# Indexer and attention scores of a hybrid decoder layer: the low product of two heads on 64 rows each

## The chip, the cores and the metric

The kernel runs on one core of a Trainium2 chip. The metric is the device time of one execution in microseconds; lower is better. The kernel before took 1328.76 us, the median of 3 runs (1328.71 to 1334.23).

A core has TensorE (PE, matrix products; its weight loads are listed as PEld), VectorE (DVE), ScalarE (ACT), GpSimd (POOL), and SyncE (SP), which issues the DMAs here. Products land in PSUM banks, from which ACT and DVE read.

## The reference

One decoder layer on 1024 tokens with 16 learned meta tokens ahead, width 1024. A root-mean-square norm feeds one input projection, whose columns go to two mixers side by side: chunkwise retention with 4 heads, and sparse attention. Their outputs are concatenated and projected, added to the input, and a squared-ReLU MLP follows. Everything is float32. The part that matters here is the sparse attention, block by block of 128 queries:

```python
s = einsum('bchd,bsd->bchs', iqb, ikf)              # indexer: 8 heads of 64, one shared key
score = einsum('bch,bchs->bcs', iwb, relu(s))       # weighted sum over the heads
_, sel = top_k(where(causal, score, NEG), 256)      # 256 keys for each query
logits = einsum('bchd,bckd->bchk', qb, k_sel)       # attention: 8 heads of 64, shared keys
p = softmax(where(valid, logits + bias, NEG))       # bias by distance, 32 buckets
out = einsum('bchk,bckd->bchd', p, v_sel)
```

## The kernel before

**Two halves.** Each float32 operand of a large product is split into a high half (rounded to the reduced format fp32r that PE takes) and a low half (the rest). A projection is then three products: high x high, low x high, high x low (L229 to L231).

**Stacked scores.** The heads of the indexer and of the attention have 64 entries, half of PE's 128 rows, so the kernel stacks. The key tiles hold the high half twice, in rows 0-63 and 64-127 (`ikh`, `knh`), and likewise the low half (`ikl`, `knl`; `stacks`, L273 to L275). A query tile of one head has its high half in one set of 64 rows and its low half in the other. Which is where alternates: for even heads the high half is in rows 0-63, for odd heads in rows 64-127 (L317 to L323 for the indexer, L529 to L534 for the attention). One product with the high keys gives q_high·k_high + q_low·k_high. A second one with the low keys, into the same bank, adds q_high·k_low + q_low·k_low.

**Indexer.** `index(i, st)` (L325 to L341) runs for the query blocks 1 to 7. For each of 8 heads it goes over chunks of the 16 + 128(i+1) keys (one chunk up to 512 columns, then 2 or 3 near-equal ones): two products into one of the five banks of the pool "R" (`psB`, L332 and L333), a ReLU on ACT that scales by the head's weight (L335), and a signed sum into `sc[i]` on DVE (L337, L339). Per head, the seven blocks have 272 + 400 + 528 + 656 + 784 + 912 + 1040 = 4,592 columns in 13 chunks.

**Top-k.** It runs bit by bit on DVE and ACT, beside the retention (183 to 421 us). Afterwards `sc[i]` holds 0-or-large penalties in place of scores.

**Attention.** `attend_p(i, g)` takes block i and four heads. For each head it goes over the segments of the keys: the last 240 (with the distance bias) and the chunks before. Each segment is two products into one of three banks of the pool "A" (`psA`, L554 and L555), and one DVE operation that adds the bias or penalty and takes the minimum (L556). After the last segment comes the exponential on ACT (L563), and a `yield`, four in a call. Per head, the eight blocks have 144 + 4,592 = 4,736 columns in 18 segments. `attend_v` transposes the exponentials (L581), splits them (L587, L588) and multiplies by the values (L589, L590) with banks of the pool "R". Its first step covers only the 16 meta tokens, so that its two products have 16 rows; all other steps have 128.

**Order.** `spread` interleaves the generators of one step (scores of a unit, values of the unit before, pieces of the output projection L640 to L642) by their yields. On top of that the program is given to a planner that simulates the engines with a cost model and puts on each engine, in program order of priority, what is ready first. Each engine then runs its list in that order. The DMAs stand in SP's list.

**Memory.** `shift(pool, n)` takes n bytes of each partition out of a pool by a buffer that is only cleared once (L122).

Of the kernel before, what the change touches and what calls it, by code (L numbers as in the profile page):

```python
# [9 lines left out]
F32 = mybir.dt.float32  # L10
# [3 lines left out]
AF = mybir.ActivationFunctionType  # L14
ALU = mybir.AluOpType
# [55 lines left out]
def chunks(n, c0=0):  # L71
    k = -(-n // 512)
    out = []
    for j in range(k):
        a, b = (n * j // k) // 64 * 64, (n * (j + 1) // k) // 64 * 64 if j + 1 < k else n
        out.append((c0 + a, b - a))
    return out
# [3 lines left out]
def layer(ctx, tc, x, meta, norm1_w, w_in, ret_w, q_w, k_w, rel, w_out, norm2_w, w1, w2,  # L81
          ident_d, pack_d, hot_d, out, gam):
    nc = tc.nc
    const = ctx.enter_context(tc.tile_pool(name="const", bufs=1))
    wp = ctx.enter_context(tc.tile_pool(name="wp", bufs=1))
    small = ctx.enter_context(tc.tile_pool(name="small", bufs=2))
# [10 lines left out]
    def psA():  # L97
        return pp.tile([128, 512], F32, tag="A", name="psA", bufs=3)

    def psB():  # L100
        return pp.tile([128, 512], F32, tag="R", name="psB", bufs=5)
# [18 lines left out]
    def shift(pool, n):  # L120

        nc.gpsimd.memset(pool.tile([128, n // 4], F32, name="shift", bufs=1), 0.0)  # L122

    shift(const, 128)
    shift(small, 224)
    ident = const.tile([128, 128], F32, name="ident")
    nc.sync.dma_start(ident, ident_d)
    nrow = const.tile([128, D], F32, name="nrow", tag="nrow")
# [33 lines left out]
    ikl = px.tile([128, KW], F32R, name="ikl")  # L162
# [122 lines left out]


    ncol = [NM + 128 * (i + 1) for i in range(NB)]
    sc = [None] * NB

    def sc_tile(i, shape, dt, name):  # L290
        return kp_.tile(shape, dt, tag=f"sc{i}", name=name)
# [33 lines left out]

    def index(i, st):
        sc[i] = sc_tile(i, [128, ncol[i]], F32, "sc")
        for h in range(8):
            for c0, w in chunks(ncol[i]):
                dst = sc[i][:, c0:c0 + w]  # L330
                ps = psB()
                nc.tensor.matmul(ps[:, :w], st[:, h], ikh[:, c0:c0 + w], start=True, stop=False)  # L332
                nc.tensor.matmul(ps[:, :w], st[:, h], ikl[:, c0:c0 + w], start=False, stop=True)  # L333
                r = big.tile([128, 512], F32, tag="oh", name="rl", bufs=3)
                nc.scalar.activation(r[:, :w], ps[:, :w], AF.Relu, scale=absw[:, i, h:h + 1])  # L335
                if h == 0:
                    nc.vector.tensor_scalar(dst, r[:, :w], sgnw[:, i, h:h + 1], None, op0=ALU.mult)  # L337
                else:
                    nc.vector.scalar_tensor_tensor(dst, r[:, :w], sgnw[:, i, h:h + 1], dst, op0=ALU.mult, op1=ALU.add)  # L339
        diag = sc[i][:, ncol[i] - 128:]  # L340
        nc.gpsimd.affine_select(diag, diag, pattern=[[-1, 128]], compare_op=ALU.is_ge, fill=-BIG,  # L341
                                base=0, channel_multiplier=1)
# [9 lines left out]
    ps = psA()  # L352
# [10 lines left out]
    for b in range(NB):  # L363
        if b + 2 < NB:
            do_norm1(b + 2)
        sb = small_proj(b, sh, sl)
        key_T([(sb[:, 0:64], 128)], NM + 128 * b, ikh, ikl)
        if b == 0:
            s8 = small_proj(8, sh, sl)
            key_T([(s8[:NM, 0:64], NM)], 0, ikh, ikl)  # L370
        if b:
            index(b, index_q(b))
# [24 lines left out]
    knh = ap_.tile([128, KW], F32R, name="knh")  # L397
    knl = ap_.tile([128, KW], F32R, name="knl")
    bias = ap_.tile([128, 8, WIN], F32, name="bias")
    kr = rsqrt(kss, 9)  # L400
    for b in range(9):
        P = NM if b == 8 else 128
# [22 lines left out]
    st = {}  # L425
# [64 lines left out]
    for b in range(NB):  # L490
        ps = psA()
# [16 lines left out]
    segs = {}  # L508
    wins = {i: min(ncol[i], WIN) for i in range(NB)}
    for i in range(NB):  # L510
        n = ncol[i]
        win = wins[i]
        segs[i] = [(c0, w, False) for c0, w in chunks(n - win)] + [(n - win, win, True)]
    qst = {}
# [21 lines left out]
    def attend_p(i, g):  # L536
        n = ncol[i]
        win = wins[i]
        mb = at["m"][:, g]
        u = 2 * i + g  # L540
        nc.gpsimd.tensor_tensor(mb[:, :, :win], bias[:, 4 * g:4 * g + 4, WIN - win:],
                                sc[i][:, None, n - win:].to_broadcast([128, 4, win]), op=ALU.add)
        P = []
        sums = small.tile([128, 4], F32, name="sums")
        rs = small.tile([128, 4], F32, name="rs")
        for hh in range(4):
            per = 4 if i < 3 else 2
            if hh % per == 0:
                pp2 = (page if u < 4 or u % 4 >= 2 and i >= 3 else page_b)([128, per, n if i < 7 else 1056], F32, "P")
            p = pp2[:, hh % per]  # L550
            mn = small.tile([128, len(segs[i])], F32, name="mn", tag=f"mn{len(segs[i])}")
            for k, (c0, w, last) in enumerate(segs[i]):
                ps = psA()
                nc.tensor.matmul(ps[:, :w], qst[i][:, 4 * g + hh, :], knh[:, c0:c0 + w], start=True, stop=False)  # L554
                nc.tensor.matmul(ps[:, :w], qst[i][:, 4 * g + hh, :], knl[:, c0:c0 + w], start=False, stop=True)  # L555
                nc.vector.tensor_tensor_reduce(  # L556
                    out=p[:, c0:c0 + w], in0=ps[:, :w], in1=mb[:, hh, :win] if last else sc[i][:, c0:c0 + w],
                    scale=1.0, scalar=3e38, op0=ALU.add, op1=ALU.min, accum_out=mn[:, k:k + 1])
            m1 = mn
            if len(segs[i]) > 1:  # L560
                m1 = small.tile([128, 1], F32, name="m1")
                nc.vector.tensor_reduce(m1, mn, axis=mybir.AxisListType.X, op=ALU.min)
            nc.scalar.activation(p[:, :n], p[:, :n], AF.Exp, scale=-1.0, bias=m1, accum_out=sums[:, hh:hh + 1])  # L563
            P.append(p)
            yield
        nc.vector.reciprocal(rs, sums)
        res[i, g] = P, rs
# [100 lines left out]
    for h in range(4):  # L668
        st["w", h] = load_cols(w_in, [(o + 128 * h, 128) for o in (RQ, RK, RV, RG)])
        ret_meta(h)  # L670
        for c in range(NB):
            if h == 3 and c == 5:
                open_att()
                load_q(0)
            if h == 3 and c == 6:
                load_q(1)
            if h == 3 and c == 7:
                spread((4, attend_p(0, 0)))
            cur = ret_in(h, c)
            if prev:  # L680
                ret_out(*prev)
            prev = cur
    ret_out(*prev)
    spread((4, attend_p(0, 1)))


# [85 lines left out]
    for u in range(2, 2 * NB):  # L772
        i, g = u // 2, u % 2
        if g == 0 and i + 1 < NB:
            load_q(i + 1)
        work = [(4, attend_p(i, g))]
        if u == 2:
            work.append((2, attend_v(0, 0)))
        work.append(((u - 1) // 2 + 2, attend_v((u - 1) // 2, (u - 1) % 2)))
        for ch, b in pieces.get(u, ()):  # L780
            work.append((9, out_piece(ch, b)))
        spread(*work)
# [335 lines left out]
def build(nc, inputs):  # L1118
    arrays, args = {}, []

    def add(name, a):
        arrays[name] = a
        args.append(nc.dram_tensor(name, a.shape, mybir.dt.from_np(a.dtype), kind="ExternalInput").ap())
    for name in _INS:
        a = np.ascontiguousarray(inputs[name])
        if name in ("x", "w_in", "w_out", "w_ff1", "w_ff2"):
            a = a[0]
        add(f"in_{name}_dram", a)
    ident, pack, hot, gam = shape_constants()
    add("ident_dram", ident)  # L1130
    add("pack_dram", pack)
    add("hot_dram", hot)
    args.append(nc.dram_tensor("out_0_dram", (T, D), F32, kind="ExternalOutput").ap())
    with tile.TileContext(nc, schedule_with_timeline_sim=True) as tc:
        layer(tc, *args, gam)
    return arrays
# [10 lines left out]
```

## Time and profile before

| | |
|---|---|
| median of 3 runs | 1328.76 us (1328.71 to 1334.23) |
| profiled execution | 1329.52 us, its span 1327.7 us |
| granted TensorE clock, mean | 0.983 |
| PE busy | 1271.8 us, 6200 matmuls |
| PE weight loads busy | 1047.9 us, 6200 loads |
| DVE / ACT / POOL busy | 1076.9 / 750.4 / 260.8 us |

A busy share is that of the whole span. A matmul's recorded time runs to a modelled end and overlaps the next matmul's, so that the distance between two starts tells what a matmul costs in a row of them. A granted clock of 1.00 is 2.4 GHz, 0.50 is 1.2 GHz. Shapes of PE are given as rows x weight columns, then rows x moving columns: `128*128 128x512` has 128 rows and streams 512 columns, `16*128 16x512` has 16 rows.

### The profile page before, as it was taken

How to read it: one execution, taken by the hardware profiler on the slowest of the kernel's cores; microseconds unless marked ns; L12 is line 12 of the kernel's file. 1: busy time of each engine (PE TensorE's matmuls, PEld its weight loads, DVE VectorE, ACT ScalarE, POOL GpSimd, SP SyncE). 2: the span in 40 equal slices, each digit the busy share in tenths (PEclk: the TensorE clock that was granted, in tenths of full speed). 3: DMA queues.
4: the chain of work that ended last, by engine and by line, in shares of the span. 5: the costliest groups of instructions: out<-in, count | busy, mean ns of one | idle time of the engine just before them, and what ended most of it. 6: DMA issues, size and time to landing. Idle time of an engine off the chain costs nothing. (4 is left out here: it accounts for less than half of the span.)

```text
span 1327.7 us, 18666 instructions
## 1 busy us (share of the span) xinstructions
PE 1271.8 (96%) x6200; PEld 1047.9 (79%) x6200; DVE 1076.9 (81%) x2387; ACT 750.4 (57%) x1593; POOL 260.8 (20%) x297
## 2 busy tenths in 40 slices
PE   6999999899899999999997999999999999999998
PEld 5888868687777778787775888888888888888887
DVE  5678999899979878676759877777878988887875
ACT  6676647577753667565756555555556444444442
POOL 4004472323434424220343000000000200000000
PEclk9999999899999899999998999999999999999999
DMA  9103040202201211212362434434538844434222
GB/s 283 57 17 90 33 133 9 72 11 71 64 16 49 95 64 49 67 45 72 112 213 88 156 130 161 148 129 173 175 135 298 334 160 159 158 134 184 96 95 96
DMA packets 93664, 153.74 MB, mean 116 GB/s; under 512 B 7240, under 2 KB 47344, under 8 KB 89856
## 3 DMA queue, kind: packets, MB, share of 16 engines
q1 hardware_dynamic: 93568, 152.56, 33.5%
q8 instruction: 49, 0.80, 0.2%
q14 instruction: 47, 0.39, 0.1%
HBM read 110.58 MB, written 43.46 MB: 116 GB/s over the span
## 5 line engine op out<-in xcount | busy, mean ns | idle before, releaser
L898 ACT ACTIVATE wh<-ga 128x512 fp32r<-128x512 f32 x144 | 87.2, 628 | 158.7 <-PE psB L1046 141.5
L229 PE MATMUL psA<-wh,uh 128*128 128x512 f32 x376 | 152.4, 406 | 4.4 <-DVE gs L455 4.3
L231 PE MATMUL psA<-wl,uh 128*128 128x512 f32 x376 | 150.4, 400 | 0.0
L230 PE MATMUL psA<-wh,ul 128*128 128x512 f32 x376 | 150.1, 399 | 0.0
L899 DVE TENSOR_TENSOR wl<-ga,wh 128x512 fp32r<-128x512 f32 x144 | 96.7, 687 | 47.4 <-ACT wh L898 46.8
L898 ACT ACTIVATE wh<-sum 128x512 fp32r<-128x512 f32 x128 | 78.6, 625 | 74.3 <-DVE sum L895 69.9
L1046 PE MATMUL psB<-wh,wl 128*128 128x512 f32 x280 | 108.9, 389 | 0.0
L1047 PE MATMUL psB<-wl,wh 128*128 128x512 f32 x280 | 108.9, 389 | 0.0
L1045 PE MATMUL psB<-wh 128*128 128x512 f32 x280 | 106.8, 389 | 0.0
L689 DVE TENSOR_SCALAR_CACHE_REDUCE jk_cnt<-sc,tcand 128x400 bf16<-128x400 f32 (+1 forms) x124 | 102.2, 824 | 1.0
L694 ACT ACTIVATE jk_top<-sc,tcand 128x272 bf16<-128x272 f32 (+2 forms) x93 | 85.0, 914 | 28.2 <-DVE tcand L728 23.6
L899 DVE TENSOR_TENSOR wl<-sum,wh 128x512 fp32r<-128x512 f32 x128 | 87.7, 685 | 6.4 <-ACT wh L898 4.7
L229 PEld LDWEIGHTS psA<-wh,uh 128*128 128x128 f32 x376 | 72.2, 192 | 19.0 <-issue 3.5
L191 POOL TENSOR_TENSOR wl<-wr,wh 128x512 fp32r<-128x512 f32 x56 | 80.9, 1460 | 31.2 <-PE psB L641 15.5
L965 POOL COPY ga<-wl 128x1 f32<-128x1 f32 x8 | 6.6, 826 | 401.6 <-PE psB L928 276.2
L231 PEld LDWEIGHTS psA<-wl,uh 128*128 128x128 f32 x376 | 71.9, 191 | 14.4
L230 PEld LDWEIGHTS psA<-wh,ul 128*128 128x128 f32 x376 | 72.4, 192 | 13.5
L587 ACT ACTIVATE ph<-psB 128x512 fp32r<-128x512 f32 (+1 forms) x88 | 51.3, 592 | 48.3 <-PE psB L581 40.3
L588 DVE TENSOR_TENSOR ph<-psB,ph 128x512 fp32r<-128x512 f32 (+1 forms) x88 | 59.4, 683 | 17.4 <-ACT ph L587 15.9
L335 ACT ACTIVATE rl<-psB,absw 128x320 f32<-128x320 f32 (+5 forms) x104 | 52.7, 554 | 36.4 <-PE psB L333 23.9
L1046 PE MATMUL psA<-wh,wl 128*128 128x512 f32 x168 | 65.4, 389 | 0.0
L1047 PE MATMUL psA<-wl,wh 128*128 128x512 f32 x168 | 65.4, 389 | 0.0
(354 smaller groups left out, 3669.9 us busy)
## 6 DMA issues: line engine op xcount, KB each, us to landing
ga<-hid SPq DMA_DIRECT2D x28, 1024.0 KB, 4.9
wr<-in_w_ff_dram SPq DMA_DIRECT2D x34, 512.0 KB, 4.8
hid<-hs SPq DMA_DIRECT2D x48, 256.0 KB, 2.0
wr<-in_w_in_dram SPq DMA_DIRECT2D x32, 256.0 KB, 3.2
gb<-in_w_ff_dram SPq DMA_DIRECT2D x8, 1024.0 KB, 4.9
ga<-in_w_ff_dram SPq DMA_DIRECT2D x8, 1024.0 KB, 5.6
wr<-in_w_out_dram SPq DMA_DIRECT2D x12, 512.0 KB, 3.8
xt<-in_x_dram SPq DMA_DIRECT2D x8, 512.0 KB, 4.6
```

The source lines that it names most:

```text
L191: (nc.vector if alt and altc[0] % 2 else nc.gpsimd).tensor_tensor(shl, raw, shp.bitcast(F32), op=ALU.subtract)
L229: nc.tensor.matmul(ps[:P, :n], uh, wh, start=d == 0, stop=False)
L230: nc.tensor.matmul(ps[:P, :n], ul, wh, start=False, stop=False)
L231: nc.tensor.matmul(ps[:P, :n], uh, wl, start=False, stop=d == 7)
L588: nc.vector.tensor_tensor(pl[:kp], tp[:kp], ph[:kp].bitcast(F32), op=ALU.subtract)
L689: nc.vector.tensor_scalar(jk_[:, :ncol[i]], sc[i], cand[:, j:j + 1], 0.0, op0=ALU.is_ge, op1=ALU.add, accum_out=cnt[:, j:j + 1])
L694: nc.scalar.activation(jk_top[:, :ncol[i]], sc[i], AF.Sign, scale=-1.0, bias=cand[:, j:j + 1], accum_out=cnt[:, j:j + 1])
L898: nc.scalar.activation(view(hi), s, AF.Copy)
L899: nc.vector.tensor_tensor(view(lo), s, view(hi).bitcast(F32), op=SUB)
L1045: nc.tensor.matmul(ps[tb], ah[:, t], bh, start=j == 0 and m not in CONT, stop=False, skip_group_check=True)
L1046: nc.tensor.matmul(ps[tb], al[:, t], bh, start=False, stop=False, skip_group_check=True)
L1047: nc.tensor.matmul(ps[tb], ah[:, t], bl, start=False, stop=j == NO - 1, skip_group_check=True)
```

## The change

The second product of each chunk keeps only the 64 rows that hold the query's high half, so that q_low·k_low is no longer added. Two neighbouring heads, whose high halves lie in different sets of rows, are taken together: both high products, then both low products, then both evacuations. The second bank of a pair comes from the pool "R", in the attention too. In the attention the minima get four buffers in place of two, a yield moves into the middle of a pair's segments, and the two exponentials of a pair follow each other. The filler of the pool `small` shrinks by 192 bytes.

```diff
-    shift(small, 224)
+    shift(small, 32)
...
+    def half(h):
+
+        return slice(64 * (h % 2), 64 * (h % 2) + 64)
...
-        for h in range(8):
-            for c0, w in chunks(ncol[i]):
-                dst = sc[i][:, c0:c0 + w]
-                ps = psB()
+        for h2, c0, w in [(h, c0, w) for h in range(0, 8, 2) for c0, w in chunks(ncol[i])]:
+            dst = sc[i][:, c0:c0 + w]
+            pss = [psB(), psB()]
+            for h, ps in zip((h2, h2 + 1), pss):
                 nc.tensor.matmul(ps[:, :w], st[:, h], ikh[:, c0:c0 + w], start=True, stop=False)
-                nc.tensor.matmul(ps[:, :w], st[:, h], ikl[:, c0:c0 + w], start=False, stop=True)
+            for h, ps in zip((h2, h2 + 1), pss):
+                a = half(h)
+                nc.tensor.matmul(ps[:, :w], st[a, h], ikl[a, c0:c0 + w], start=False, stop=True)
+            for h, ps in zip((h2, h2 + 1), pss):
                 r = big.tile([128, 512], F32, tag="oh", name="rl", bufs=3)
...
-        for hh in range(4):
+        for h2 in (0, 2):
...
-            p = pp2[:, hh % per]
-            mn = small.tile([128, len(segs[i])], F32, name="mn", tag=f"mn{len(segs[i])}")
+            heads = [(hh, 4 * g + hh, pp2[:, hh % per], small.tile([128, len(segs[i])], F32, name="mn", tag=f"mn{len(segs[i])}",
+                                                                   bufs=4)) for hh in (h2, h2 + 1)]
             for k, (c0, w, last) in enumerate(segs[i]):
-                ps = psA()
-                nc.tensor.matmul(ps[:, :w], qst[i][:, 4 * g + hh, :], knh[:, c0:c0 + w], start=True, stop=False)
-                nc.tensor.matmul(ps[:, :w], qst[i][:, 4 * g + hh, :], knl[:, c0:c0 + w], start=False, stop=True)
-                nc.vector.tensor_tensor_reduce(
...
+                pss = [psA(), psB()]
+                for (hh, h, p, mn), ps in zip(heads, pss):
+                    nc.tensor.matmul(ps[:, :w], qst[i][:, h, :], knh[:, c0:c0 + w], start=True, stop=False)
+                for (hh, h, p, mn), ps in zip(heads, pss):
+                    a = half(h)
+                    nc.tensor.matmul(ps[:, :w], qst[i][a, h, :], knl[a, c0:c0 + w], start=False, stop=True)
+                for (hh, h, p, mn), ps in zip(heads, pss):
+                    nc.vector.tensor_tensor_reduce(
...
+                if k == (len(segs[i]) - 1) // 2:
+                    yield
+            for hh, h, p, mn in heads:
...
+                nc.scalar.activation(p[:, :n], p[:, :n], AF.Exp, scale=-1.0, bias=m1, accum_out=sums[:, hh:hh + 1])
+                P.append(p)
             yield
```

## Rows read from the trace of the kernel before

**Rows 1.** The page: busy time, share of the span, instructions.
```profile
PE 1271.8 (96%) x6200; PEld 1047.9 (79%) x6200; DVE 1076.9 (81%) x2387; ACT 750.4 (57%) x1593; POOL 260.8 (20%) x297
```

**Rows 2.** Busy time by stage: indexer, retention, attention; columns in the first line.
```profile
core 0: us, PE busy (x) PEld busy (x) DVE busy (x) ACT busy (x) POOL busy (x), PEclk, DMA share, GB/s
...
44.00:183.00 139.00, 136.22 (x742) 116.34 (x740) 117.74 (x245) 89.78 (x198) 48.49 (x43) 1.00 0.19 60
183.00:421.00 238.00, 222.80 (x1117) 183.01 (x1116) 221.60 (x678) 150.54 (x407) 83.83 (x122) 0.96 0.15 45
421.00:640.00 219.00, 210.56 (x1187) 169.07 (x1186) 165.63 (x554) 140.03 (x306) 65.41 (x46) 0.98 0.20 66
```

**Rows 3.** PE's waits in those three stages: us in total, times, longest.
```profile
PE psB L332 <- ACT rl L335: 2.4, 3, 1.0
...
PE psB L475 <- DVE sm L472: 10.0, 5, 3.6
...
PE psA L554 <- DVE mn L556: 1.9, 4, 0.8
```

**Rows 4.** Timeline of PE, plain runs: start us, us, instruction, shape.
```profile
672.19 0.39 PE L641 MATMUL psB<-wh,ys 128*128 128x512 f32 x1
672.41 0.39 PE L642 MATMUL psB<-wl,ys 128*128 128x512 f32 x1
672.64 0.39 PE L640 MATMUL psB<-wh,ys 128*128 128x512 f32 x1
...
106.44 0.34 PE L333 MATMUL psB<-ikl,iq 128*128 128x384 f32 x1
106.62 0.35 PE L332 MATMUL psB<-ikh,iq 128*128 128x400 f32 x1
...
486.35 0.27 PE L554 MATMUL psA<-knh,qs 128*128 128x240 f32 x1
486.46 0.27 PE L555 MATMUL psA<-knl,qs 128*128 128x240 f32 x1
```

**Rows 5.** The second products by line: count, ns min/median/max, first and last start, forms.
```profile
L333 PE MATMUL psB<-ikl,iq x104: 279/316/376, 44.8 to 182.6; 128*128 128x400 f32 x24, 128*128 128x320 f32 x24, 128*128 128x272 f32 x16, 128*128 128x256 f32 x8
...
L555 PE MATMUL psA<-knl,qs x144: 262/278/420, 421.0 to 613.1; 128*128 128x240 f32 x56, 128*128 128x288 f32 x16, 128*128 128x416 f32 x16, 128*128 128x144 f32 x8
```

**Rows 6.** Groups by line and form, the 16-row products: count, busy, mean ns, idle.
```profile
L590 PE MATMUL psB<-ph,vv 16*128 16x512 f32 x16 | 8.2, 515 | 0.1
L589 PE MATMUL psB<-ph,vv 16*128 16x512 f32 x16 | 8.2, 511 | 1.7 <-ACT ph L587 1.7
```

**Rows 7.** Timeline of PE around a 16-row product.
```profile
586.64 0.34 PE L555 MATMUL psA<-knl,qs 128*128 128x416 f32 x1
586.91 0.49 PE L589 MATMUL psB<-ph,vv 16*128 16x512 f32 x1
587.33 0.50 PE L640 MATMUL psB<-wh,ys 128*128 128x512 f32 x1
587.67 0.39 PE L641 MATMUL psB<-wh,ys 128*128 128x512 f32 x1
```

**Rows 8.** Weight loads at the same place, and their waits from 421 to 640 us.
```profile
586.91 0.18 PEld L589 LDWEIGHTS psB<-ph,vv 16*128 16x128 f32 x1 [0.27 <-ACT ph L587]
587.33 0.19 PEld L640 LDWEIGHTS psB<-wh,ys 128*128 128x128 f32 x1 [0.24 <-issue]
587.44 0.19 PEld L641 LDWEIGHTS psB<-wh,ys 128*128 128x128 f32 x1
...
PEld psB L640 <- issue: 1.9, 8, 0.2
```

**Rows 9.** Timeline of PE in the indexer, a chunk among projections.
```profile
49.07 0.41 PE L229 MATMUL psA<-wh,uh 128*128 128x512 f32 x1
49.32 0.28 PE L332 MATMUL psB<-ikh,iq 128*128 128x272 f32 x1
49.44 0.29 PE L333 MATMUL psB<-ikl,iq 128*128 128x272 f32 x1
49.57 0.40 PE L230 MATMUL psA<-wh,ul 128*128 128x512 f32 x1
```

**Rows 10.** DVE's groups for a chunk: indexer (44 to 183 us), attention.
```profile
L339 DVE SCALAR_TENSOR_TENSOR sc<-rl,sgnw,sc 128x320 f32<-128x320 f32 (+5 forms) x84 | 52.7, 664 | 9.8 <-ACT rl L335 8.8
...
L556 DVE CUSTOM_DVE_ANT_0 P<-psA,mb 128x240 f32<-128x240 f32 x56 | 22.5, 402 | 6.9 <-PE psA L555 6.7
```

**Rows 11.** Busy time and granted clock from 441 to 449 us; PE just before.
```profile
441.00:449.00 8.00, 8.00 (x30) 6.48 (x30) 5.17 (x23) 2.58 (x7) 1.64 (x1) 0.50 0.30 98
...
438.31 0.49 PE L589 MATMUL psB<-ph,vv 16*128 16x512 f32 x1
...
439.20 0.26 PE L555 MATMUL psA<-knl,qs 128*128 128x32 f32 x1
439.39 0.53 PE L590 MATMUL psB<-ph,vv 16*128 16x512 f32 x1
```

More of the change, by code (lines that the diff above doesn't have):

```diff
@@ L545, in attend_p @@
         rs = small.tile([128, 4], F32, name="rs")
-        for hh in range(4):
+        for h2 in (0, 2):
             per = 4 if i < 3 else 2
-            if hh % per == 0:
+            if h2 % per == 0:
                 pp2 = (page if u < 4 or u % 4 >= 2 and i >= 3 else page_b)([128, per, n if i < 7 else 1056], F32, "P")
-            p = pp2[:, hh % per]
-            mn = small.tile([128, len(segs[i])], F32, name="mn", tag=f"mn{len(segs[i])}")
+            heads = [(hh, 4 * g + hh, pp2[:, hh % per], small.tile([128, len(segs[i])], F32, name="mn", tag=f"mn{len(segs[i])}",
+                                                                   bufs=4)) for hh in (h2, h2 + 1)]
@@ L552, in attend_p @@
             for k, (c0, w, last) in enumerate(segs[i]):
-                ps = psA()
-                nc.tensor.matmul(ps[:, :w], qst[i][:, 4 * g + hh, :], knh[:, c0:c0 + w], start=True, stop=False)
-                nc.tensor.matmul(ps[:, :w], qst[i][:, 4 * g + hh, :], knl[:, c0:c0 + w], start=False, stop=True)
-                nc.vector.tensor_tensor_reduce(
-                    out=p[:, c0:c0 + w], in0=ps[:, :w], in1=mb[:, hh, :win] if last else sc[i][:, c0:c0 + w],
-                    scale=1.0, scalar=3e38, op0=ALU.add, op1=ALU.min, accum_out=mn[:, k:k + 1])
@@ L559, in attend_p @@
[L559 to L564, printed above, removed]
+                pss = [psA(), psB()]
+                for (hh, h, p, mn), ps in zip(heads, pss):
+                    nc.tensor.matmul(ps[:, :w], qst[i][:, h, :], knh[:, c0:c0 + w], start=True, stop=False)
@@ new lines, in attend_p @@
+                for (hh, h, p, mn), ps in zip(heads, pss):
[3 more added lines that the diff above has]
+                    nc.vector.tensor_tensor_reduce(
+                        out=p[:, c0:c0 + w], in0=ps[:, :w], in1=mb[:, hh, :win] if last else sc[i][:, c0:c0 + w],
+                        scale=1.0, scalar=3e38, op0=ALU.add, op1=ALU.min, accum_out=mn[:, k:k + 1])
@@ L565, in attend_p @@
+                if k == (len(segs[i]) - 1) // 2:
+                    yield
+            for hh, h, p, mn in heads:
+                m1 = mn
+                if len(segs[i]) > 1:
+                    m1 = small.tile([128, 1], F32, name="m1")
+                    nc.vector.tensor_reduce(m1, mn, axis=mybir.AxisListType.X, op=ALU.min)
+                nc.scalar.activation(p[:, :n], p[:, :n], AF.Exp, scale=-1.0, bias=m1, accum_out=sums[:, hh:hh + 1])
+                P.append(p)
             yield
```

## The prediction

> **What bounds the kernel now.** I read the page's busy times first, then the busy times by stage, then TensorE's order of time around the places that change. TensorE (PE) is busy for 96% of the span, VectorE (DVE) for 81% [rows 1]. The change touches two stages: the indexer's scores (44 to 183 us) and the attention's (421 to 640 us). In them PE is busy for 136.2 of 139 us and 210.6 of 219 us [rows 2], and the waits for a score bank that stop it there are short: 2.4 us in the indexer, 1.9 us in the attention [rows 3]. PE has other matmuls to put in (projections, transposes, the output projection), so 0.1 us of PE time in these stages is 0.1 us of the kernel. Between them, 183 to 421 us, PE leaves 15.2 of 238 us idle, 10.0 of it waiting for one DVE product of the retention [rows 2, 3]; there DVE decides too (221.6 of 238 us).
>
> A matmul's recorded time overlaps the next one's, so I use the distance from start to start. In a plain run a matmul hands over after 0.22 to 0.23 us at 512 columns, 0.18 at 384 and 0.11 at 240 [rows 4]. That is columns at 2.4 GHz plus 0.014 us. I take 0.11 as the least, the distance of two weight loads of 128 columns; the next load runs under the present matmul.
>
> **What the change removes.** Only the second product of each score chunk shrinks, from 128 rows to 64, and it keeps its columns. There are 104 such products in the indexer (L333) and 144 in the attention (L555) [rows 5], and the code gives their columns: 8 heads x 4,592 = 36,736 and 8 x 4,736 = 37,888. Indexer: 36,736 columns at 2.4 GHz is 15.3 us, plus 104 x 0.014 = 1.5, so 16.8 us. Attention: 24 of the chunks (32, 144, 160 columns) cost the 0.11 of a load, 2.6 us; the other 120 with 35,200 columns cost 14.7 + 1.7 us; 19.0 us together. The second products thus take 35.8 us. Fewer rows don't make a product shorter: one of 16 rows and 512 columns is recorded with 511 ns [rows 6], beside 0.39 for 128 rows [rows 7]. Something is saved only if the halves of two heads, one on rows 0-63 and one on rows 64-127, run at the same time. Then half goes: 17.9 us, or 0.144 us for each of the 124 pairs (52 + 72). That is all that the change can win.
>
> **What it adds.** The trace has matmuls on few rows: 32 in the attention's value product (the 16 meta tokens, 16 each on L589 and L590) [rows 6], each alone among 128-row ones. I read their price from start to start [rows 7]. L555 of 416 columns starts at 586.64 and should hand over after 0.19; the 16-row L589 starts at 586.91, 0.08 late. The next, L640, starts 0.42 later in place of 0.23, and the one after that 0.34 later in place of 0.23. From 586.64 to 587.67 it is 1.03 us where 0.19 + 0.23 + 0.23 = 0.65 would do: 0.38 us for one excursion to 16 rows and back. The weight loads show why [rows 8]: L640's load begins not under the 16-row product but 0.42 us after that product's own load, after 0.24 us of idle put down to "issue" (the same idle stands before eight loads of L640), and the 16-row load had not gone ahead either. So each change of row count empties the array (about 0.09 us) and then loads weights in the open (about 0.10 us), twice.
>
> In the changed order each pair and chunk is: high, high (128 rows), low, low (64 rows), then 128 rows again. That is one excursion per pair, 124 in place of none, if the four matmuls stay together. No row shows 64 rows, nor two row halves side by side. Bounds per excursion: if the halves overlap wholly and their loads too, 0.38 - 0.144 = +0.24 us; if the halves overlap but the second load follows the first 0.11 later, +0.35; if they don't overlap, +0.38. I take 0.35, since the loads of 128 columns start 0.11 us apart there (587.33 and 587.44 [rows 8]). The lower bound of the whole edit is a switch that costs nothing at 64 rows, -0.144 us.
>
> The Trainium skill has a rule for the step from 16 rows to 64 ("TensorEngine Tiling (Array Packing)", Key Properties): changing the tiling mode, not just the tile, drains the engine. The trace agrees at 16 rows (0.08 us late on entry); no run here shows 64. By the rule the sum is the one below; without it, the lower bound stays open.
>
> **Pairs that fall apart.** The planner sets the order and takes what is ready first. The two high products need two free banks at once. Before, a chunk may stand alone between other work, as the one at 49.32, between two projection matmuls [rows 9]. Where the second bank comes later, the first head's low product goes ahead alone, and the pair makes two excursions with nothing side by side: 2 x 0.38 = 0.76 us. DVE needs 0.66 us for a chunk of the indexer [rows 10] against 0.3 of PE, so banks come free one by one there. Bounds: none of the pairs, all of them. I take a sixth, 21 pairs (9 + 12): a whole pair is the planner's first choice wherever two banks are free.
>
> **The sum.** Indexer: 43 x 0.35 + 9 x 0.76 = 21.9 us of PE. Attention: 60 x 0.35 + 12 x 0.76 = 30.1 us. The attention's part I count in full, as PE has no slack there. Of the indexer's I take 7 us as absorbed by the 15.2 us that PE leaves idle in the next stage; bounds are nothing and 15. Total 21.9 - 7 + 30.1 = 45 us. The profiled execution took 1329.52 us (span 1327.7), the median of the runs shown is 1328.76; 1329.5 + 45 = 1374.5, less the 0.8 between them: 1374 us.
>
> The rest I cost at nothing. ACT, DVE and POOL do the same operations on the same shapes. The second head's evacuation starts one low product later than now; the banks in between cover it, and without cover it is some 0.3 us per pair, the excursion again. Two heads' exponentials come together on ACT, which is busy for 57% [rows 1]. Attention moves 72 of its 144 banks to the pool that transposes and sums use. If each waited for a DVE evacuation (0.40 us at 240 columns [rows 10]) it would be 29 us more; less load on its own pool can give back the 1.9. A call hands over to neighbouring work four times, as before. The smaller filler is one memset on a POOL that is 20% busy. DMAs and their queues stay.
>
> **Rivals.**
> - *The halves run together and 64 rows cost no switch.* Then 17.9 us go: 1311 us. It wins as long as an excursion costs under 0.144 us. For it: each half keeps to its own rows and its own bank, and 0.38 is measured on 16 rows. Against it: the price is paid on the way in and on the way out, whichever matmul follows. Chance 0.08. The Trainium skill speaks for the first half of this ("TensorE: Matmul & The Clock Gate", Part 3: Packing small matmuls): matmuls on different row groups overlap, about 4 ns apart. No row here shows it; with [rows 7] it leads to the +0.24 above.
> - *About nothing.* The switch to 64 rows costs 0.15 to 0.20 us, half of that to 16: 124 x (0.15 to 0.20, less 0.144) is 1 to 7 us, 1329 to 1336 us. For: half the rows stay. Against: the same as above. Chance 0.08.
> - *All pairs fall apart.* 248 excursions x 0.38 = 94 us, less 10 absorbed: 1413 us. For: [rows 9] and DVE's 0.66 [rows 10]. Against: attention draws its banks from two pools. Chance 0.10.
> - *The clock falls as well.* PE was granted half clock, 0.50, from 441 to 449 us, after a stretch with two such excursions within 1.1 us and chunks of 32 columns [rows 11]. If 60 us more of score work ran at 1.2 GHz, 30 us would come on top of the forecast: 1404 us. Against: the indexer and the later attention have long 128-row runs between. Chance 0.10.
> - The forecast (excursions paid, pairs mostly whole): 0.64, with its own range 1350 to 1395, from +0.24 per pair with none split (30 us, less 8) to a third split at 0.38 and 0.76 (63 us).
>
> **How the numbers follow.** 0.5%, 6.6 us, is about what this kernel's times can tell from no change. Slower: 0.64 + 0.10 + 0.10 and a little of "about nothing", 0.85. Same 0.07, faster 0.08. The range goes down to 1334, past the forecast's low end and into "about nothing", and up to 1412, which takes in the fallen clock and nearly all pairs split.
>
> **What would show it.** Right: the low products' loads begin only when the high products are done, with idle "issue" ahead of the load that follows the pair; from the start of a pair's first low product to the start of the next 128-row one some 0.44 us at 300 columns (the 0.42 of [rows 7], less 0.09 for the shorter stream, plus the second load), where two products take 0.28 now; both score stages longer, with DVE's and ACT's busy time unchanged. Wrong: the second low product starting with the first and the next load under it; or a longer time with PE waiting for banks, no longer the one waited for.

## The result, and the profile after

The change made the kernel slower: 1434.03 us (median of 4 runs, 1431.33 to 1436.92), a ratio of 1.0789 to the kernel before, 95% interval 1.0746 to 1.0833. That is 105 us more; 45 were forecast, and the range ended at 1412 us. The profiled execution's span grew from 1327.7 to 1429.5 us, 101.8 us.

The busy line of the page after stands beside that of before [rows 1]:

```profile
PE 1372.2 (96%) x6200; PEld 1075.2 (75%) x6200; DVE 1082.2 (76%) x2387; ACT 756.5 (53%) x1593; POOL 256.0 (18%) x297
```

PE is busy for 100 us more with as many matmuls; DVE and ACT do what they did. So the loss is PE's. Next the stages of after: indexer's scores, retention, attention up to the first matmul of the MLP.

```profile
core 0: us, PE busy (x) PEld busy (x) DVE busy (x) ACT busy (x) POOL busy (x), PEclk, DMA share, GB/s
43.00:220.00 177.00, 177.00 (x752) 122.30 (x750) 127.80 (x265) 94.48 (x200) 46.59 (x47) 0.95 0.16 47
220.00:451.00 231.00, 218.30 (x1101) 180.48 (x1101) 217.75 (x662) 150.95 (x405) 81.98 (x119) 0.96 0.16 47
451.00:800.00 349.00, 328.75 (x1456) 236.70 (x1455) 206.90 (x604) 177.52 (x375) 91.87 (x73) 0.91 0.21 70
```

The kernel before, cut at the same places (first and last stage):

```profile
45.00:182.00 137.00, 134.57 (x733) 114.98 (x731) 116.54 (x241) 88.78 (x196) 48.49 (x43) 1.00 0.19 60
421.00:698.00 277.00, 263.59 (x1455) 211.54 (x1454) 203.67 (x607) 177.22 (x374) 91.57 (x74) 0.98 0.28 89
```

Indexer 137 to 177 us, attention 277 to 349 us, retention between them 239 to 231 us. The MLP is as long as before. The granted clock also fell, in the attention from 0.98 to 0.91 and in the indexer from 1.00 to 0.95. At two levels, 1.00 and 0.50, this is 18% of the attention at 1.2 GHz in place of 4%, and 10% of the indexer in place of none, though PE is recorded there without a gap. One stretch of the changed kernel's indexer at 1.2 GHz, and PE just before and in it:

```profile
86.00:96.00 10.00, 10.00 (x27) 6.50 (x27) 4.37 (x10) 4.53 (x11) 0.00 (x0) 0.50 0.00 0
...
84.62 0.39 PE L337 MATMUL psB<-ikh,iq 128*128 128x272 f32 x1
84.94 0.39 PE L340 MATMUL psB<-ikl,iq 64*128 64x272 f32 x1
85.26 0.38 PE L337 MATMUL psB<-ikh,iq 128*128 128x256 f32 x1
...
88.00 0.59 PE L337 MATMUL psB<-ikh,iq 128*128 128x272 f32 x1
88.53 0.59 PE L340 MATMUL psB<-ikl,iq 64*128 64x272 f32 x1
89.05 0.58 PE L337 MATMUL psB<-ikh,iq 128*128 128x256 f32 x1
```

Two products of 272 columns, a high one and a low one that stands alone, take 0.64 us from start to start before the fall and 1.05 us in it. Both stages together have about 70 us more at 1.2 GHz than before; if all of it slows as these two products do, that is 27 of the 105 us, an estimate.

What PE does in a score chunk of the indexer at 2.4 GHz, matmuls and weight loads in order of time:

```profile
110.46 0.19 PEld L337 LDWEIGHTS psB<-ikh,iq 128*128 128x128 f32 x1 [0.16 <-ACT rl L343]
110.46 0.42 PE L337 MATMUL psB<-ikh,iq 128*128 128x336 f32 x1
110.81 0.18 PEld L340 LDWEIGHTS psB<-ikl,iq 64*128 64x128 f32 x1 [0.16 <-issue]
110.81 0.42 PE L340 MATMUL psB<-ikl,iq 64*128 64x336 f32 x1
111.15 0.19 PEld L337 LDWEIGHTS psB<-ikh,iq 128*128 128x128 f32 x1 [0.17 <-ACT rl L343]
111.16 0.42 PE L337 MATMUL psB<-ikh,iq 128*128 128x336 f32 x1
```

The order is high, low, high, low, not high, high, low, low. Each low product stands alone; its load starts with it, not under the product ahead. A chunk of 336 columns takes 0.70 us from start to start, where two plain products of that width take 0.31 (336 / 2.4 GHz + 0.014, twice): 0.39 us for the trip, the price read from the 16-row products [rows 7].

In the planned order of the whole kernel, 90 of the indexer's 104 low products and all 144 of the attention's stand alone. Only 7 of 124 pairs stayed together. The trips to 64 rows number 90 + 7 + 144 = 241. One of the seven whole pairs, PE in order of time:

```profile
128.02 0.64 PE L337 MATMUL psB<-ikh,iq 128*128 128x400 f32 x2
128.59 0.45 PE L340 MATMUL psB<-ikl,iq 64*128 64x400 f32 x2
128.97 0.44 PE L337 MATMUL psB<-ikh,iq 128*128 128x384 f32 x1
129.34 0.44 PE L340 MATMUL psB<-ikl,iq 64*128 64x384 f32 x1
129.71 0.50 PE L229 MATMUL psA<-wh,uh 128*128 128x512 f32 x1
```

The two low products of 400 columns (x2) hand over after 0.38 us; a single one of 384 columns takes 0.37. The second is free: both halves of the rows, loads included, run at the same time.

### The profile page after: what moved, and what is told of

It is laid out like the page before. It is cut to its first block, busy times and chain, and to the rows that moved or that the text cites. A ratio compares the mean times of both kernels' runs of the same rounds, so it can differ in the third digit from the quotient of the medians.

```text
span 1429.5 us, 18582 instructions
## 1 busy us (share of the span) xinstructions
PE 1372.2 (96%) x6200; PEld 1075.2 (75%) x6200; DVE 1082.2 (76%) x2387; ACT 756.5 (53%) x1593; POOL 256.0 (18%) x297
## 5 line engine op out<-in xcount | busy, mean ns | idle before, releaser
L343 ACT ACTIVATE rl<-psB,absw 128x400 f32<-128x400 f32 (+7 forms) x104 | 56.6, 555 | 58.8 <-PE psB L340 52.1
L191 POOL TENSOR_TENSOR wl<-wr,wh 128x512 fp32r<-128x512 f32 x56 | 77.9, 1409 | 30.7 <-PE psB L656 14.1
L347 DVE SCALAR_TENSOR_TENSOR sc<-rl,sgnw,sc 128x400 f32<-128x400 f32 (+7 forms) x91 | 56.2, 627 | 26.6 <-ACT rl L343 24.7
```

## The experiments

Each ratio is against runs of the kernel before on the same chip, made beside the experiment's own. Where two experiments with different runs of the kernel before are set against each other, it is by their ratios, times 1328.8 us.

**1. Whole pairs.** An order edge, which tells the planner that one instruction comes after another, puts both low products behind the second high product, in the indexer and likewise in the attention:

```diff
             for h, ps in zip((h2, h2 + 1), pss):
-                nc.tensor.matmul(ps[:, :w], st[:, h], ikh[:, c0:c0 + w], start=True, stop=False)
+                hi = nc.tensor.matmul(ps[:, :w], st[:, h], ikh[:, c0:c0 + w], start=True, stop=False)
-            for h, ps in zip((h2, h2 + 1), pss):
-                a = half(h)
-                nc.tensor.matmul(ps[:, :w], st[a, h], ikl[a, c0:c0 + w], start=False, stop=True)
+            with tc.issue_after(hi.ins):
+                for h, ps in zip((h2, h2 + 1), pss):
+                    a = half(h)
+                    nc.tensor.matmul(ps[:, :w], st[a, h], ikl[a, c0:c0 + w], start=False, stop=True)
```

> The changed kernel with an order edge that keeps the two low products of a pair behind both of its high products, so that a pair makes one trip to 64 rows. In the changed kernel 7 pairs stood together and 117 fell apart, 241 trips; here 125. Theory A (each trip to 64 rows and back costs some 0.38 us, and the two halves run side by side when they stand together, so a whole pair costs 0.38 - 0.14 = 0.24 us more than before): 125 x 0.24 = 30 us, a little of it absorbed, 1345 to 1362 us. Rival B (the extra time comes from the pair structure: the pool shared with the transposes, the later evacuation): no better than the changed kernel, above 1410 us. Rival C (the halves don't run side by side): 125 x 0.38 = 48 us, 1370 to 1380 us.

1394.15 us, ratio 1.0482 (1.0434 to 1.0529). All 52 pairs of the indexer and 71 of 72 in the attention were whole, and 41 us of the 105 went; 64 stayed, twice what theory A allowed. So pairs falling apart was a cause, and there was another. The order suggests why pairs fall apart: even under the edge, the two high products stood next to each other in only 27 of the 52 pairs of the indexer and 3 of 72 in the attention (three places with one bank of each pool and the same columns). The second bank comes later, and without the edge the first low product then goes ahead. This is read from the order; no run gave the pairs more banks.

**2. Pairs on 128 rows.** One line of the changed kernel; the 6200 matmuls stand in the same order in both traces, and the banks are the same.

```diff
     def half(h):
-        return slice(64 * (h % 2), 64 * (h % 2) + 64)
+        return slice(0, 128)
```

> The changed kernel, same instructions in the same order and the same banks, but the low products on all 128 rows again. Theory A (the time is the trips to 64 rows): back to the kernel before, 1325 to 1335 us. Rival B (pair structure and shared pool): stays near 1434 us; a mixture lies between, and its distance from 1329 is B's share.

1357.62 us, ratio 1.0200 (1.0158 to 1.0242). Neither theory alone: with not one trip to 64 rows the kernel is 2.0% slower than before, 27 us, and the 64 rows cost the other 5.9%, 78 us. The trace puts the 27 us into the attention, 303 us in place of 277 (the indexer is 6 us longer, the retention 4 shorter):

```profile
425.00:728.00 303.00, 277.48 (x1453) 222.29 (x1452) 200.95 (x603) 176.46 (x374) 90.78 (x73) 0.92 0.25 81
```

PE is idle there for 25.5 us, before for 13.4, and the clock falls to 0.92. PE's largest wait in that stretch is the value product's, for ACT's copy of the transposed exponentials (us in total, times, longest); first the kernel before, in its attention stage, then this one, then the changed kernel:

```profile
PE psB L589 <- ACT ph L587: 3.9, 6, 1.2
```

```profile
PE psB L604 <- ACT ph L602: 16.6, 14, 2.8
```

```profile
PE psB L604 <- ACT ph L602: 14.1, 12, 2.4
```

**3. Rows alone.** The kernel before, one head after the other with its own banks, with 64 rows in the low products (shown for the indexer; the attention has the same edit):

```diff
-                nc.tensor.matmul(ps[:, :w], st[:, h], ikl[:, c0:c0 + w], start=False, stop=True)
+                a = slice(64 * (h % 2), 64 * (h % 2) + 64)
+                nc.tensor.matmul(ps[:, :w], st[a, h], ikl[a, c0:c0 + w], start=False, stop=True)
```

> The kernel before, with nothing changed but the 64 rows of the low products: one head after the other, its own banks as before, 248 trips. Theory A: 248 x 0.385 us = 95 us, plus what the clock loses, 1420 to 1440 us, as slow as the changed kernel. Rival B: near 1330 us.

1407.77 us, ratio 1.0582 (1.0536 to 1.0628): 77 us. The 248 trips make 0.31 us each of kernel time, less than 0.385. The indexer's stage grew by 41 us for 104 trips (0.40 each); the attention's by 40 us for 144 (0.28), where PE's idle time fell from 13.4 to 7.8 us, and the retention gave 5 us back. The sum of the rows alone (5.8%) and the pairs on 128 rows (2.0%) is the change's 7.9%.

**4. Both products on the same rows.** Whole pairs, but `a = half(0)` for both heads, so that the odd heads' low product takes the query's low half. The edit to experiment 1, in the indexer and in the attention:

```diff
-                    a = half(h)
+                    a = half(0)
```

> As the order of whole pairs, but both heads' low products on rows 0 to 63, so that the odd heads' product takes the query's low half in place of its high half. Theory A (only different halves of the rows run side by side): the second product follows the first, a pair costs 0.38 us more than before, 125 x 0.38 = 48 us, some 18 us slower than whole pairs on both halves: 1365 to 1385 us. If 64-row products overlap wherever they lie (rival): the same time as whole pairs.

1416.25 us, ratio 1.0640 (1.0593 to 1.0686), 21 us above whole pairs; the level is higher than expected, as in whole pairs, but the difference is the one forecast. A pair of 400 columns, first on different rows, then on the same:

```profile
119.57 0.45 PE L341 MATMUL psB<-ikl,iq 64*128 64x400 f32 x2
119.95 0.50 PE L230 MATMUL psA<-wh,ul 128*128 128x512 f32 x1
```

```profile
121.29 0.62 PE L341 MATMUL psB<-ikl,iq 64*128 64x400 f32 x2
121.84 0.45 PE L337 MATMUL psB<-ikh,iq 128*128 128x384 f32 x1
```

0.38 us against 0.55. The difference is one product, so two overlap because of where their rows lie. Over the 123 whole pairs, 0.17 us each makes the 21 us.

**5. Pairs on 128 rows, banks from pool A.** Experiment 2, with the attention's banks as below.

```diff
-                pss = [psA(), psB()]
+                pss = [psA(), psA()]
```

> The pairs on 128 rows again (26 us slower than the kernel before), now with both banks of an attention pair from the attention's own pool A; the indexer as there. Theory D (the pair structure costs because attention takes banks of pool R from the transposes and sums of the value product, which then run less far ahead, so that TensorE waits for ScalarE's copies): most of the 26 us go, what stays is the indexer's 6: 1331 to 1341 us. Rival E (the yields in the middle of a pair and the two exponentials one after the other delay the value product): stays at 1350 to 1360 us.

1323.10 us, ratio 0.9971 (0.9948 to 0.9993). All of the 27 us went and 4 more. The attention's stage took 273 us, PE's wait for ACT's copies fell from 16.6 to 2.3 us and the clock was back at 0.98:

```profile
PE psB L604 <- ACT ph L602: 2.3, 5, 0.8
```

```profile
418.00:691.00 273.00, 260.80 (x1451) 210.48 (x1450) 200.36 (x605) 177.05 (x374) 91.68 (x73) 0.98 0.28 89
```

**6. The shared pool alone.** The kernel before; only the odd heads' banks in the attention come from pool R.

```diff
-                ps = psA()
+                ps = psB() if hh % 2 else psA()
```

> The kernel before, one head after the other on 128 rows, with one edit: the odd heads' score banks in the attention come from pool R. Theory D: 15 to 25 us slower than before, 1345 to 1357 us. Rival E: within 5 us of before, 1327 to 1337 us.

1373.78 us, ratio 1.0335 (1.0306 to 1.0365), 45 us: more than theory D asked for. The same wait is on top, at 23.3 us, and the clock is at 0.91:

```profile
PE psB L589 <- ACT ph L587: 23.3, 16, 2.2
```

```profile
420.00:740.00 320.00, 284.64 (x1447) 225.23 (x1447) 204.91 (x608) 176.28 (x374) 90.96 (x74) 0.91 0.24 77
```

So it is the pool, not the yields or the order of the exponentials. The traces also show the transposes running less far ahead: when a value product starts, 2.1 sets of transposes that are still to be used have begun, its own among them (mean of 88), in the kernel before and in experiment 5, against 1.8 in the changed kernel and experiment 2, and 1.7 here. Why it costs more with single heads than with pairs was not tried.

**7. The price of a trip at another place.** The kernel before; the value product's step over the 16 meta tokens takes all 128 rows, with the rows that don't count zeroed.

```diff
+    nc.vector.tensor_scalar(vv[:, 8], nrow[:, :128], 0.0, None, op0=ALU.mult)
...
-            nc.tensor.matmul(pv, vv[:kp, b, :], ph[:kp], start=k == 0, stop=False)
-            nc.tensor.matmul(pv, vv[:kp, b, :], pl[:kp], start=False, stop=k == len(tiles) - 1)
+            nc.tensor.matmul(pv, vv[:, b, :], ph, start=k == 0, stop=False)
+            nc.tensor.matmul(pv, vv[:, b, :], pl, start=False, stop=k == len(tiles) - 1)
```

> The kernel before, with the value product's step over the 16 meta tokens on all 128 rows: rows 16 to 127 of the values are zeroed, and the exponentials' halves hold older numbers there. It takes away 32 trips to 16 rows and changes no score product. Theory A (a trip costs 0.38 us wherever it stands): 32 x 0.38 = 12 us faster, 1317 to 1323 us. Rival (trips cost only where score products pair up, or lie hidden in waits): within 4 us of before.

1323.96 us, ratio 0.9953 (0.9929 to 0.9977): 6 us faster, half of theory A's 12. The stage shows where the other half went:

```profile
420.00:690.00 270.00, 251.66 (x1454) 209.48 (x1453) 207.16 (x610) 176.57 (x374) 91.19 (x74) 0.98 0.29 91
```

PE's busy time fell by 11.9 us, as 32 x 0.38 has it, but the stage only by 7: PE's idle time in it grew from 13.4 to 18.3 us. A trip costs PE its full price; here 40% of it had stood where PE would have waited anyway. Most of the new idle time is the wait for the score banks, 1.9 us before [rows 3]:

```profile
PE psA L555 <- DVE mn L557: 5.8, 7, 3.6
```

**8. Whole pairs with pool A.** Experiment 1 with the edit of experiment 5, so that no bank of the attention's scores comes from pool R:

```diff
-                pss = [psA(), psB()]
+                pss = [psA(), psA()]
```

> Whole pairs on 64 rows (1394 us with a bank from each pool), with both banks of an attention pair from pool A. Theory A and D together: what whole pairs cost over pairs on 128 rows (37 us) on top of the pairs with pool A: 1365 to 1378 us. If the shared pool is not the cause: 1390 to 1400 us.

1353.93 us, ratio 1.0183 (1.0147 to 1.0219), below the forecast by 11 us, because pool A gave more than the 26 us that were in that sum: 40 us against experiment 1. Against experiment 5 it is 2.1%, 28 us for 126 trips (52 in the indexer, 74 in the attention): 0.22 us for a whole pair. No run has whole pairs on 128 rows, so what the order edge itself costs is in this figure. From start to start, 48 of the indexer's whole pairs, all at 2.4 GHz, took 0.24 us more than plain products of their widths would (median), which leaves little for the edge. This is the change as it was meant, and it is still slower than not changing the rows.

**9. The two gains together.** Before, with experiment 7 and, in the attention alone, experiment 5. To the lines of experiment 7 come:

```diff
-        for hh in range(4):
+        for h2 in (0, 2):
...
-                ps = psA()
+                pss = [psA(), psA()]
...
+                    a = slice(0, 128)
```

> The kernel before with two things that were faster by themselves in the attention stage: the value product's meta step on 128 rows (its stage was 7 us shorter) and the attention's scores in pairs on 128 rows with both banks from pool A (its stage was 3.5 us shorter, while the indexer in pairs was 6 us longer; here the indexer stays as before). If the two add: 10 us less than before, 1313 to 1321 us. If both fill the same idle time of TensorE: 1320 to 1326 us, no better than the value step alone.

1325.41 us, ratio 0.9962 (0.9941 to 0.9983). They don't add up to the 10 us of the sum: this is what either gives alone.

**10 and 11. Four heads on one trip.** The kernel before, its indexer by four heads: four high products, then four low ones, on 64 rows (10) or 128 (11).

```diff
+        for h4, c0, w in [(h, c0, w) for h in (0, 4) for c0, w in chunks(ncol[i])]:
...
+            with tc.issue_after(hi.ins):
+                for h, ps in grp4:
+                    a = slice(64 * (h % 2), 64 * (h % 2) + 64)    # 11: slice(0, 128)
```

> The kernel before with the indexer alone by four heads: four high products, then the four low products together on 64 rows (two on each half), 26 trips. Theory A (one trip costs 0.38 us and products on different halves run side by side): a group pays 0.38 and gets back two of four products, 2 x 0.16 = 0.32 us, so 26 x 0.06 = 1.5 us more than the same groups on 128 rows (the run beside this one); within 5 us of it. Rival (in a group of four the third product doesn't start until both first are done and loads again in the open): 26 x 0.2 to 0.4 = 5 to 10 us more.

> The same groups of four in the indexer with the low products on 128 rows: the yardstick for the run beside it. Four banks of five are wanted at once; in pairs the indexer was 6 us longer than by single heads, so 6 to 25 us slower than before, 1334 to 1353 us.

1347.51 us, ratio 1.0128 (1.0091 to 1.0165), and 1340.48 us, 1.0080 (1.0051 to 1.0109). The two intervals overlap, but the runs don't: the fastest of four on 64 rows took 1343.25 us, the slowest of eight on 128 rows 1342.90. The 7 us between the medians are more than theory A allowed and of the rival's size. Yet the rival's mechanism isn't in the trace: from its first high product to its last the indexer was only 2.7 us longer on 64 rows, and 4.8 us lie in the retention after it, where the two kernels have the same work. The granted clock was lower on 64 rows in both (0.95 against 0.97, and 0.96 against 0.98), which would be about enough for all of it; this was not tried. The timeline of PE on 64 rows shows that four go two and two:

```profile
120.34 0.34 PE L332 MATMUL psB<-ikh,iq 128*128 128x400 f32 x1
120.61 0.63 PE L336 MATMUL psB<-ikl,iq 64*128 64x400 f32 x4
121.17 0.44 PE L332 MATMUL psB<-ikh,iq 128*128 128x384 f32 x1
121.45 0.39 PE L231 MATMUL psA<-wl,uh 128*128 128x512 f32 x1
```

Four products of 400 columns take 0.56 us, a pair 0.38: the second two add one product, 0.18. With 0.09 of delay on the way in and 0.11 after, a trip of four costs 0.76 us where four plain products take 0.72. At four wide chunks the trip itself is about paid for, not more; and wanting four banks at once, under the edge, costs 0.8% by itself.

## Why the prediction was wrong

**The direction and the price were right.** A trip to fewer rows and back costs 0.38 to 0.39 us of PE where the rows above show it, on 64 rows as on 16. The rule of the Trainium skill ("TensorEngine Tiling (Array Packing)", Key Properties) that a change of mode drains the engine agrees with the trace at 64 rows: the load at 110.81 doesn't go ahead, and 0.16 us of "issue" stand before it. But the attention's price was not to be counted in full for want of slack: in experiment 3 its stage grew by 40 us where 144 x 0.385 is 55.

**"Pairs that fall apart" failed in its size.** I took a sixth of the pairs, 21; it was 117 of 124. The sum had 145 trips (103 + 42), the kernel 241. I argued that a whole pair is the planner's first choice wherever two banks are free. That may be so, but two banks are seldom free together: 7 of 52 pairs and none of 72 stayed whole, and even under the edge the high products were neighbours in 27 and 3. The row that I had, a chunk alone between projections [rows 9], and DVE's 0.66 us per chunk [rows 10] spoke for banks that come one by one; I set them against a preference that no row showed. With 234 trips alone at 0.385 and 7 whole pairs at 0.24 the term is 92 us of PE, not 52.

**The whole pair was mis-sized the other way.** I took +0.35, the second load following the first; the loads overlap too, and a whole pair costs 0.22 us (experiment 8), about the lower bound of +0.24. There were 7 of them, so this term did little here.

**"The rest I cost at nothing" failed.** Attention's 72 banks from pool R cost 27 us (experiment 2), 45 in single heads (experiment 6). The bound that I named, 29 us, was near by luck: I had the score products wait for DVE's evacuation. What waits is the value product: with fewer banks, transposes run less far ahead, and PE waits for ACT's copies (3.9 us before, 14.1 in the changed kernel, 16.6 and 23.3 in experiments 2 and 6, 2.3 without the shared pool). I looked for waits for score banks [rows 3] and not for who else lives on pool R.

**The absorbed 7 us were right in size only.** From the last high product of the indexer to the first of the attention it was 238.5 us before and 231.4 after. But PE's idle time fell by only 2.5 us there (15.2 [rows 2] to 12.7) and by 2.8 in the indexer. The rest goes with work that had moved ahead into the longer indexer stage, where DVE was busy for 127.8 us in place of 116.5.

**The rivals.** "All pairs fall apart" (1413 us, chance 0.10) was nearest, and "the clock falls as well" came beside it: about 70 us more at 1.2 GHz, where I had 60. I had kept the two apart, and the pool in neither. The range's upper end, 1412 us, stood at one of them alone. The two experiments that split the change, rows alone and pairs on 128 rows, add up to 77 + 27 = 104 us, against 105. The fallen clock is inside both of these numbers, and no run separates it.

## What to carry to other kernels

Half-row matmuls pay only if a trip to them saves more than it costs: here 0.38 us per trip, so at least four products of 400 columns on one trip, two on each half, to break even on the trip itself; the one kernel with such trips was still 7 us slower than the same groups on 128 rows. Make sure of the order first (an order edge, then a look at the planned order), since a pair that needs two banks at once fell apart here where banks came free one at a time. Before a tile moves to another pool, look at what its banks allow the other users to run ahead.

## What the runs showed of the hardware

Two 64-row products on different halves of the rows overlap completely with their weight loads: 0.38 us for a pair of 400 columns, 0.37 for one of 384, 0.55 for a pair on the same half.

The granted clock was lower where small waits were spread through the attention: 0.98 with 12 to 13 us of PE idle (before, experiment 5), 0.92 and 0.91 with 25 and 35 us (experiments 2 and 6), and these stages grew by more than their waits did. But idle time doesn't tell it. With 18 us, in experiment 7, the clock stayed at 0.98; and in the indexer it fell with no idle time recorded, after rows of 64-row products that stand alone, to 0.95 in the changed kernel and to 0.94 in experiment 3 (1.00 before):

```profile
44.00:223.00 179.00, 179.00 (x736) 123.18 (x734) 125.74 (x252) 97.66 (x202) 45.99 (x45) 0.94 0.16 47
```

So the trips lengthened the kernel by their own time and went along with a lower clock besides; what exactly brings it down was not tried.
